# Attention means of two heads taken together, and adaLN column sums taken two by two with their steps dealt out again

## The chip, the cores and the metric

One core of a Trainium2 chip runs the whole program in one launch. The metric is device time in microseconds (us). The core has TensorE (PE in the profile, with PEld for its weight loads), VectorE (DVE), ScalarE (ACT), GpSimd (POOL), SyncE (SP, which here only issues DMAs), and 16 DMA engines.

## The reference, cut to what matters

Two layers over 512 latent tokens and 256 context tokens, 1024 features, 16 heads of 64, float32. Layer 0 mixes tokens by a short gated convolution, layer 1 by neighbourhood attention; each is followed by a SwiGLU of hidden width 2816. Context tokens are carried through layer 0 only.

```
mod   = silu(c)     @ w_ada[i] + b_ada[i]      # 6 vectors of 1024: sh1 sc1 g1 sh2 sc2 g2
mod_c = silu(c_ctx) @ w_ada[i] + b_ada[i]      # the same for context tokens
h = rms_norm(x, norm_mix[i]) * (1 + sc1) + sh1
x = x + g1 * mixer(h)                          # layer 0: conv, layer 1: attention
x = x + g2 * swiglu(rms_norm(x, norm_ffn[i]) * (1 + sc2) + sh2)
# attention, for each head: latent queries on their window and on all context keys
p = softmax(concat(s_win + bias, s_ctx));  o = p_win @ v_win + p_ctx @ v_ctx
```

## The kernel before, in words

Features lie on the 128 partitions (8 tiles), tokens along the free dimension: X is the latent group (512 columns), C the context group (256). A float32 weight tile is split into two float32r parts (`split`: `wh` on ACT at L139, `wl` on DVE at L140), and so is every operand; a product is three matmuls (`mm3`, L193). `Stream` loads weight blocks of 1 MB through SP into a ring of three `raw` buffers and splits one tile ahead.

**Order.** The program is traced once; a planner then simulates it and puts each engine's instructions in an order, in which what was traced earlier goes first when it is ready in the simulation. `in_order` pins an instruction behind everything that was traced before it on its engine. An instruction that is not pinned may be put ahead of one that waits, but once the order is made an engine follows it.

**adaLN (`Ada`).** The product of silu(c) and silu(c_ctx) with w_ada is not done by large matmuls. One step loads 512 rows by 512 columns of w_ada (1 MB, into the same `raw` ring); DVE multiplies by the conditioning column and accumulates into `aa0` (L287, L289), and where context needs it too ACT multiplies (L292, L295) and POOL accumulates into `aa1` (L296). Two steps (halves of the rows) make one piece of 512 columns: half a vector. `flush` sums the piece over the partitions by matmuls against `ones2` (128 rows, 32 columns, one per condition) into 32 partitions of the bank `ada_ps` (L311). After four pieces, two vectors, `finish` copies the bank to `row` on DVE (L318), transposes it (L321), adds the bias, and makes the gains of a norm (1 + scale) * norm weight. The first two vectors of layer 0 are done apart (L241). There are 16 steps for layer 0 and 24 for layer 1 (the last 16 of these without context). In the convolution loop (f = 2 to 7) two steps follow each feature tile, four follow f = 5, and `flush` stands after the first of the three products of the next tile; all 16 are done before the `residual` of the mixer. In the SwiGLU of layer 0 one step follows each hidden tile, two in the first chunk.

**Attention.** Heads go in 8 pairs. For a query tile `b` of 128 queries (4 per pair) and a head `a` of the pair, `scores` makes one bank (L865, L866), its minimum, the bias and mask (L869, L870), the exponential `pt` (L874) and the division (L876, L877); `pt` has two buffers. `mean` transposes four 128-column pieces of `pt` (L893), copies them to `tps` on ACT (L895 to L898), and adds four matmuls of `vv` (128 keys by the 64 columns of this head) with `tps` into the 64 partitions of this head in the bank `op` (L900). At `b` 0 and 3 one of the four has 64 keys only (64 rows). A float32 matmul that isn't a transpose shows as two matmul instructions in the trace, so a head of a query tile has eight at L900. `run` takes (pair, b, a) units in turn: the scores of a unit, then the mean of the unit before, then some steps of `side`, which hold the preparation of the next pair (`operands`) and the projection of the one after (`project`), or in the last two pairs the output projection.

Of the kernel before, what the change touches and what calls it, by code (L numbers as in the profile page):

```python
# [15 lines left out]
P = 128  # L16
# [15 lines left out]
C_ID, C_IND, C_SEL, C_MASK = 0, 128, 160, 288  # L32
MASK_AT = {0: (0, 192), 1: (192, 256), 2: (192, 256), 3: (448, 192)}
C_N = C_MASK + 640
# [3 lines left out]
def dit_kernel(  # L38
# [39 lines left out]
    ct = const.tile([P, C_N], F32, name="ct")  # L78
# [4 lines left out]
    nc.vector.tensor_copy(out=sel, in_=ct[:, C_SEL:C_SEL + P])  # L83
# [12 lines left out]
    cs = const.tile([P, KT, 32], F32, name="cs")  # L96
    nc.vector.memset(cs, 0.0)
    nc.scalar.activation(out=cs[:, :, 0], in_=vt[:, V_C:V_C + KT], func=AF.Silu)
    nc.scalar.activation(out=cs[:, :, 1], in_=vt[:, V_CC:V_CC + KT], func=AF.Silu)
# [114 lines left out]
    class Ada:  # L214


        def __init__(self, pool):
            self.pool = pool
            self.steps = [(i, q, half) for i in range(2) for q in range(4 if i == 0 else 0, 12) for half in range(2)]
            self.pos, self.todo = 0, None  # L220
# [13 lines left out]
        def first_sum(self, n, part, raw):  # L234
# [3 lines left out]
            for j in range(4):  # L238
                for k in range(part * nk, part * nk + nk):
                    kk = k - part * nk  # L240
                    in_order(nc.tensor.matmul(  # L241
                        self.ps[32 * j:32 * j + 32, :wd], cs[:, k, :], raw[:, kk, j // 2, j % 2 * wd:(j % 2 + 1) * wd],
                        start=(k == 0), stop=(k == KT - 1)))
# [20 lines left out]

        def step(self, n=1):
# [5 lines left out]
        def _step(self, i, q, half):  # L271
# [5 lines left out]
            if half == 0:  # L277
                self.flush()
                self.acc = [self.pool.tile([P, 512], F32, name=f"aa{c}", tag=f"aa{c}", bufs=1) for c in range(1 + both)]
            for kk in range(4):  # L280
                k = half * 4 + kk
                for c in range(1 + both):
                    w = cs[:, k, c:c + 1]
# [15 lines left out]
            self.todo = (i, q, both, self.acc)  # L299

        def flush(self):

            if self.todo is None:
                return
            i, q, both, accs = self.todo
            self.todo = None
            j = q % 4
            if j == 0:
                self.ps = bank("ada", "ada_ps")
            for c in range(1 + both):  # L310
                nc.tensor.matmul(self.ps[32 * j:32 * j + 32, :], ones2[:, c, :], accs[c],  # L311
                                 start=(c == 0), stop=(c == both))
            if j == 3:
                self.finish(i, q // 4)

        def finish(self, i, g):
            row = nrm.tile([P, 512], F32, name="row", tag="row", bufs=1)
            nc.vector.tensor_copy(out=row, in_=self.ps)  # L318
            tp = bank("ada", "ada_tp")
            for s in range(4):  # L320
                nc.tensor.transpose(out=tp[:, s * P:(s + 1) * P], in_=row[:, s * P:(s + 1) * P], identity=ident)  # L321
            tv = tp.rearrange("p (s j m) -> p j s m", s=4, j=4)
            ba = vt[:, V_BADA + i * 48 + g * 16:V_BADA + i * 48 + g * 16 + 16].rearrange("p (j s) -> p j s", j=4)
            for cond in range(2 if i == 0 or g == 0 else 1):
                nc.vector.tensor_tensor(
                    out=mod[i][:, cond, g * 16:g * 16 + 16].rearrange("p (j s) -> p j s", j=4),
                    in0=tv[:, :, :, cond], in1=ba, op=ALU.add)
            if g == 1:
                return
            which = 0 if g == 0 else 1  # L330
            base = V_NMIX if which == 0 else V_NFFN
            at = 8 if which == 0 else 32
            gt = const.tile([P, 2, KT], F32, name=f"gain{i}{which}")
            for cond in range(2 if i == 0 or g == 0 else 1):
                nc.vector.scalar_tensor_tensor(
                    out=gt[:, cond, :], in0=mod[i][:, cond, at:at + KT], scalar=1.0,
# [110 lines left out]
    def residual(stream, i, gate, groups, srcs, norms=None, out=None, use="ada"):  # L447
# [18 lines left out]
    def swiglu(tmp, ap_, i, groups, hs, chunks, ada=None, begin=None, norms=None, out=None, end=None, begin_norm=None):  # L466
# [25 lines left out]
        for ci, n_t in enumerate(chunks):  # L492
# [43 lines left out]
            while tt < n_t:  # L536
# [9 lines left out]
                if ada is not None:  # L546
                    ada.step(1 + (ci == 0))
# [4 lines left out]
            residual(st, i, 5, groups, srcs, norms if last else None, out)  # L552
# [3 lines left out]
    with ExitStack() as l0:  # L556
        tmp = l0.enter_context(tc.tile_pool(name="tmp0", bufs=2))
        ap0 = l0.enter_context(tc.tile_pool(name="ap0", bufs=8))
        ada = Ada(tmp)
# [40 lines left out]
        def first_weights(q, j):  # L600
# [3 lines left out]
            elif j == 2:  # L604
                raw = tmp.tile([P, 512], F32, name="fraw", tag=f"aa{q - 2}", bufs=1)
# [467 lines left out]
```

## Time and profile before

| | |
|---|---|
| time, median of 3 runs | 1699.52 us (1699.45 to 1699.55) |
| profiled execution, its own time | 1700.69 us |
| its span, first to last instruction | 1698.6 us |
| PE busy | 1656.7 us (98%) |
| PEld busy | 1366.1 us (80%) |
| DVE busy | 862.5 us (51%) |
| ACT busy | 578.7 us (34%) |
| POOL busy | 245.0 us (14%) |
| mean granted TensorE clock | 0.991 |
| DMA | 162.41 MB, mean 96 GB/s |

Busy is the time in which an engine has at least one instruction under way; for PE that says little about how fast it goes, since matmuls overlap and their ends are modelled. How far apart they start says more.

### The profile page before, as it was taken

Reading aid. Unit: us, or ns where it says so; the run is one execution under the profiler, and the core shown is the slowest. Engines: PE = TensorE matmul, PEld = TensorE weight load, DVE = VectorE, ACT = ScalarE, POOL = GpSimd, SP = SyncE. Lnnn points to the kernel's source line nnn. Section 1 sums busy time; section 2 is a strip of 40 time slices with the busy share of each in tenths; the row PEclk is TensorE's granted clock in tenths of the full one; section 3 lists DMA queues with packets and bytes.
Section 4 is the critical chain, followed back from the end, with each engine's and each line's share of the span. In section 5 each row is a group of like instructions: output and inputs, shape, how many; then the busy total and the mean of one; then the engine's idle time right before and its main releaser. Section 6 shows DMA issues by size and latency. Waiting matters only on the chain.

```text
span 1698.6 us, 22136 instructions
## 1 busy us (share of the span) xinstructions
PE 1656.7 (98%) x9128; PEld 1366.1 (80%) x9128; DVE 862.5 (51%) x1390; ACT 578.7 (34%) x973; POOL 245.0 (14%) x282
## 2 busy tenths in 40 slices
PE   6999989999999999999999999999999999999999
PEld 5887767888788888888888777777778888888887
DVE  5656777267844443234332756555667633333333
ACT  4343333244411211112222555555545522222221
POOL 0134444214500000000003201111120100000000
PEclk9999999999999999999999999999999999999999
DMA  9433434204533333123321211110112023233321
GB/s 303 132 104 122 147 124 149 75 25 150 169 112 101 114 124 124 50 100 124 100 75 50 66 47 57 32 57 26 50 62 82 26 99 111 88 100 99 100 81 68
DMA packets 137076, 162.41 MB, mean 96 GB/s; under 512 B 3216, under 2 KB 114064, under 8 KB 136976
## 3 DMA queue, kind: packets, MB, share of 16 engines
q1 hardware_dynamic: 133504, 156.66, 28.4%
q10 hardware_dynamic: 3472, 4.34, 0.8%
q8 instruction: 71, 1.16, 0.3%
q14 instruction: 29, 0.24, 0.0%
HBM read 158.90 MB, written 2.10 MB: 95 GB/s over the span
## 4 chain that ended last, share of the span: by engine, by line
PE 89%; DVE 7%; DMA 1%; issue 1%; ACT 1%; POOL 0%; SPq 0%; POOLq 0%; DVEq 0%; ACTq 0%
PE ps L193 76%; PE op L900 4%; DVE aa L289 3%; PE tp L893 2%; PE ada_ps L311 2%; DVE wl L140 1%; DMA raw<-in_w_ada_dram 1%; PE s L865 1%; PE ada_ps L241 1%; PE s L866 1%; PE stt L787 1%; DVE al L140 0%; DVE t L426 0%; PE bc L410 0%; DVE hxl L429 0%
## 5 line engine op out<-in xcount | busy, mean ns | idle before, releaser
L193 PE MATMUL ps<-hxh,wh 128*128 128x512 f32 (+1 forms) x1128 | 440.2, 396 | 3.2 <-ACT hxh L428 1.7
L193 PE MATMUL ps<-hxl,wh 128*128 128x512 f32 (+1 forms) x1128 | 434.7, 391 | 1.4 <-DVE hxl L429 1.3
L193 PE MATMUL ps<-hxh,wl 128*128 128x512 f32 (+1 forms) x1128 | 433.6, 390 | 2.4 <-DVE wl L140 2.4
L139 ACT CAST wh<-raw 128x1024 fp32r<-128x1024 f32 (+1 forms) x194 | 198.1, 1023 | 480.4 <-PE ps L193 424.8
L140 DVE TENSOR_TENSOR wl<-raw,wh 128x1024 fp32r<-128x1024 f32 (+1 forms) x194 | 241.0, 1244 | 157.7 <-ACT wh L139 148.0
L193 PEld LDWEIGHTS ps<-hxh,wh 128*128 128x128 f32 x1128 | 212.1, 189 | 66.3 <-issue 10.2
L193 PEld LDWEIGHTS ps<-hxh,wl 128*128 128x128 f32 x1128 | 212.9, 189 | 48.9 <-DVE wl L140 3.5
L193 PEld LDWEIGHTS ps<-hxl,wh 128*128 128x128 f32 x1128 | 212.7, 189 | 46.6 <-DVE hxl L429 3.6
L193 PE MATMUL ps<-ah,wh 128*128 128x512 f32 (+1 forms) x656 | 231.4, 353 | 0.0
L193 PE MATMUL ps<-al,wh 128*128 128x512 f32 (+1 forms) x656 | 230.7, 352 | 0.0
L193 PE MATMUL ps<-ah,wl 128*128 128x512 f32 (+1 forms) x656 | 230.4, 352 | 0.0
L193 PE MATMUL ps<-hch,wl 128*128 128x256 f32 x648 | 181.3, 284 | 0.0
L193 PE MATMUL ps<-hcl,wh 128*128 128x256 f32 x648 | 181.0, 284 | 0.0
L193 PE MATMUL ps<-hch,wh 128*128 128x256 f32 x648 | 179.7, 284 | 0.0
L296 POOL TENSOR_TENSOR aa<-aa,pr 128x512 f32<-128x512 f32 x84 | 132.1, 1573 | 119.5 <-ACT pr L295 62.7
L442 DVE SCALAR_TENSOR_TENSOR x<-ps,mod,x 128x512 f32<-128x512 f32 (+1 forms) x80 | 55.2, 696 | 178.7 <-PE ps L193 178.7
L289 DVE SCALAR_TENSOR_TENSOR aa<-raw,cs,aa 128x512 f32<-128x512 f32 x140 | 139.1, 994 | 7.8 <-DMA raw<-in_w_ada_dram 5.0
L193 PEld LDWEIGHTS ps<-ah,wh 128*128 128x128 f32 x656 | 123.4, 188 | 18.8 <-ACT ah L139 0.8
L193 PEld LDWEIGHTS ps<-ah,wl 128*128 128x128 f32 x656 | 123.4, 188 | 17.5
L193 PEld LDWEIGHTS ps<-al,wh 128*128 128x128 f32 x656 | 123.4, 188 | 17.5
L383 POOL TENSOR_TENSOR acc<-acc,sq 128x256 f32<-128x256 f32 (+1 forms) x40 | 45.9, 1147 | 587.1 <-ACT sq L381 536.6
L485 DVE TENSOR_TENSOR sg<-ps,sg 128x512 f32<-128x512 f32 x66 | 39.7, 601 | 177.2 <-PE ps L193 175.6
(171 smaller groups left out, 1840.1 us busy)
## 6 DMA issues: line engine op xcount, KB each, us to landing
raw<-in_ffn_w_in_dram SPq DMA_DIRECT2D x44, 1024.0 KB, 5.1
raw<-in_w_ada_dram SPq DMA_DIRECT2D x40, 1024.0 KB, 5.1
raw<-in_ffn_w_out_dram SPq DMA_DIRECT2D x16, 1024.0 KB, 4.9
raw<-in_attn_w_qkv_dram SPq DMA_DIRECT2D x12, 1024.0 KB, 5.2
raw<-in_conv_w_in_dram SPq DMA_DIRECT2D x9, 1024.0 KB, 5.2
raw<-in_w_ada_dram SPq DMA_DIRECT2D x16, 512.0 KB, 8.0
raw<-in_ffn_w_out_dram SPq DMA_DIRECT2D x8, 768.0 KB, 4.4
raw<-in_conv_w_out_dram SPq DMA_DIRECT2D x4, 1024.0 KB, 5.2
```

What stands on the lines that cost most here:

```text
L139: a = pinned(nc.scalar.copy(out=hi, in_=src))
L140: b = pinned(nc.vector.tensor_tensor(out=lo, in0=src, in1=hi.bitcast(F32), op=ALU.subtract))
L193: m = nc.tensor.matmul(ps, w[k][part], src[k], start=(first and k == i == 0), stop=(last and k == nk - 1 and i == 2))
L241: in_order(nc.tensor.matmul(self.ps[32 * j:32 * j + 32, :wd], cs[:, k, :], raw[:, kk, j // 2, j % 2 * wd:(j % 2 + 1) * wd], start=(k == 0) ...
L289: nc.vector.scalar_tensor_tensor(out=acc, in0=raw[:, kk, :], scalar=w, in1=acc, op0=ALU.mult, op1=ALU.add)
L296: nc.gpsimd.tensor_tensor(out=acc, in0=acc, in1=pr, op=ALU.add)
L311: nc.tensor.matmul(self.ps[32 * j:32 * j + 32, :], ones2[:, c, :], accs[c], start=(c == 0), stop=(c == both))
L383: eng.tensor_tensor(out=self.a, in0=self.a, in1=sq, op=ALU.add)
L442: nc.vector.scalar_tensor_tensor(out=grp.tiles[f], in0=ps, scalar=modv(i, grp.cond, gate, f), in1=grp.tiles[f], op0=ALU.mult, op1=ALU.add)
L485: nc.vector.tensor_tensor(out=sg, in0=pu[:, :n], in1=sg, op=ALU.mult)
L893: nc.tensor.transpose(out=tp[0:p1, j * P:(j + 1) * P], in_=pt[:, c0:c0 + p1], identity=ident)
L900: nc.tensor.matmul(op_[own, 0:P], vv[p0:p1, vi, own], tps[p0:p1, j * P:(j + 1) * P], start=(j == 0), stop=(j == 3))
```

## The change

Four edits. (1) In attention a unit is now (pair, b) with both heads: both scores, then both heads' transposes (`turned`), one side step, then 8 matmuls in which the heads alternate, each pinned. The 64-row pieces at b = 0 and 3 become full 128-row ones: a value tile with zeros in its other half is added to `vv` (one more transpose per pair). (2) A `flush` waits for two pieces, and their matmuls alternate between the two 32-partition strips, pinned; one vector is then finished alone (10 finishes instead of 5), its bank copied on ACT (64 partitions), with pinned transposes of 64 columns. The accumulators have two sets. (3) The steps are dealt out again: in the convolution one per tile (two at f = 2), four in the mixer's `residual`, the rest along the SwiGLU of layer 0 and in its residuals. In the convolution the flush stands after the second product. (4) `cs` and the raw form of `sel` move to buffers that are reused later.

```diff
-    def residual(stream, i, gate, groups, srcs, norms=None, out=None, use="ada"):
+    def residual(stream, i, gate, groups, srcs, norms=None, out=None, use="ada", along=None):
...
+            if along and f in along:
+                along[f]()
...
+        def also(self):
+            self.flush()
+            self.step()
...
-                self.acc = [self.pool.tile([P, 512], F32, name=f"aa{c}", tag=f"aa{c}", bufs=1) for c in range(1 + both)]
+                self.acc = [self.pool.tile([P, 512], F32, name=f"aa{c}", tag=f"aa{c}{q % 2}", bufs=1) for c in range(1 + both)]
...
-            self.todo = (i, q, both, self.acc)
+            self.todo.append((i, q, both, self.acc))
...
-            if self.todo is None:
+            if len(self.todo) < 2:
                 return
...
             for c in range(1 + both):
-                nc.tensor.matmul(self.ps[32 * j:32 * j + 32, :], ones2[:, c, :], accs[c],
-                                 start=(c == 0), stop=(c == both))
-            if j == 3:
-                self.finish(i, q // 4)
+                for j, (_, _, _, accs) in enumerate(two):
+                    in_order(nc.tensor.matmul(self.ps[32 * j:32 * j + 32, :], ones2[:, c, :], accs[c],
+                                              start=(c == 0), stop=(c == both)))
+            self.finish(i, q // 2)
...
-            nc.vector.tensor_copy(out=row, in_=self.ps)
+            nc.scalar.copy(out=row[0:64, :], in_=self.ps[0:64, :])
             tp = bank("ada", "ada_tp")
             for s in range(4):
-                nc.tensor.transpose(out=tp[:, s * P:(s + 1) * P], in_=row[:, s * P:(s + 1) * P], identity=ident)
+                in_order(nc.tensor.transpose(out=tp[:, s * 64:(s + 1) * 64], in_=row[0:64, s * P:(s + 1) * P],
+                                             identity=ident[0:64, 0:64]))
...
-                ada.step(1 + (ci == 0))
+                ada.step()
...
+            along = {0: ada.also, 2: ada.also, 4: ada.also, 6: ada.flush} if ada is not None and not last else None
+            residual(st, i, 5, groups, srcs, norms if last else None, out, along=along)
...
-        ada.step(2)
+        ada.step()
...
-                if j == 0:
+                if j == 1:
                     ada.flush()
...
-            ada.step(4 if f == 5 else 2)
-        ada.flush()
+            ada.step(2 if f == 2 else 1)
...
-        residual(st, 0, 2, groups, srcs, norms, hs[0])
+        residual(st, 0, 2, groups, srcs, norms, hs[0], along={0: ada.also, 1: ada.also, 2: ada.also, 3: ada.also, 5: ada.flush})
...
+            nc.gpsimd.memset(edge[:, 64:128], 0.0)
+            nc.gpsimd.tensor_copy(out=edge[:, 128:192], in_=vx[:, NX - 64:NX])
...
+            for s, src in enumerate((edge[:, 64:64 + P], v_sb[:, 0:P], v_sb[:, P:2 * P])):
+                nc.tensor.transpose(out=t2[:, s * P:(s + 1) * P], in_=src, identity=ident)
...
+        def turned(b, pt):
+
+            tp = bank("tp", "tp")
+            tps = pa.tile([P, 512], F32, name="tps", tag="tps")
+            for j, (c0, vi) in enumerate(TILES[b]):
+                nc.tensor.transpose(out=tp[:, j * P:(j + 1) * P], in_=pt[:, c0:c0 + P], identity=ident)
+            nc.scalar.copy(out=tps, in_=tp)
+            return tps
+
+        def mean(r, b, tps, op_):
+
+            vv = r["ops"][3]
+            for j, (c0, vi) in enumerate(TILES[b]):
+                for a in range(2):
+                    own = slice(64 * a, 64 * a + 64)
+                    in_order(nc.tensor.matmul(op_[own, 0:P], vv[:, vi, own], tps[a][:, j * P:(j + 1) * P],
+                                              start=(j == 0), stop=(j == 3)))
...
-                    pts[u] = scores(pairs[units[u][0]], *units[u][1:])
+                    pts[u] = [scores(pairs[units[u][0]], units[u][1], a) for a in range(2)]
                 if u > 0:
...
+                    pr, b = units[u - 1]
+                    tps = [turned(b, pt) for pt in pts.pop(u - 1)]
+                    if pos < len(side):
+                        next(side[pos], None)
+                        pos += 1
+                    op_ = bank("op", "op")
+                    mean(pairs[pr], b, tps, op_)
...
-                while pos < min(pace(u), len(side)):
+                while pos < min(pace(2 * u + 1), len(side)):
```

## Rows read from the trace of the kernel before

**Rows 1.** The chain that ended last: its shares of the span by line.
```profile
by line: PE ps L193 76.1%; PE op L900 3.9%; DVE aa L289 2.7%; PE tp L893 1.8%; PE ada_ps L311 1.7%; issue 1.3%; DVE wl L140 1.2%; DMA raw<-in_w_ada_dram 1.2%; PE s L865 1.2%; PE ada_ps L241 1.2%; PE s L866 0.9%; PE stt L787 0.6%; DVE al L14
```

**Rows 2.** Tiles op, ada_ps: matmuls, count, shortest/median/longest ns, first and last start.
```profile
L900 PE MATMUL op<-tps,vv x512: 269/273/324, 1001.5 to 1323.5; 128*64 128x128 f32 x150, 64*64 64x128 f32 x21
...
L311 PE MATMUL ada_ps<-aa,ones x64: 592/617/1062, 71.7 to 839.5; 128*32 128x512 f32 x64
```

**Rows 3.** Timeline of PE, attention of one pair: start, length (us), what.
```profile
1059.70 1.58 PE L900 MATMUL op<-tps,vv 128*64 128x128 f32 x16
...
1069.97 0.28 PE L193 MATMUL ps<-hch,wh 128*128 128x256 f32 x1
1070.18 1.09 PE L900 MATMUL op<-tps,vv 128*64 128x128 f32 x8
1071.20 0.39 PE L193 MATMUL ps<-hcl,wh 128*128 128x256 f32 x1
1071.42 0.28 PE L193 MATMUL ps<-hch,wl 128*128 128x256 f32 x1
1071.54 0.27 PE L193 MATMUL ps<-hch,wh 128*128 128x256 f32 x1
```

**Rows 4.** The stretch of 16 at 1059.70, L900 alone, by windows: matmuls under way (x).
```profile
1059.69:1060.18 0.49, 0.48 (x4) 0.48 (x5) 1.00 0.00 0
1060.18:1060.62 0.44, 0.44 (x10) 0.44 (x9) 1.00 0.00 0
```

**Rows 5.** Timeline of PE: sums of three 32-column matmuls in three strips.
```profile
1073.77 0.62 PE L787 MATMUL stt<-sq,ct 128*32 128x512 f32 x2
1073.78 0.62 PE L787 MATMUL stt<-sqc,ct 128*32 128x512 f32 x1
...
1074.76 0.50 PE L865 MATMUL s<-ks,qh 128*128 128x512 f32 x1
```

**Rows 6.** Timeline of PE around adaLN sums (L311), at three places.
```profile
135.53 1.91 PE L311 MATMUL ada_ps<-aa,ones 128*32 128x512 f32 x2 [3.29 <-DVE aa L289]
...
138.39 0.63 PE L193 MATMUL ps<-hxh,wl 128*128 128x512 f32 x1
138.82 0.63 PE L193 MATMUL ps<-hxh,wh 128*128 128x512 f32 x1
...
287.08 1.90 PE L311 MATMUL ada_ps<-aa,ones 128*32 128x512 f32 x4
...
540.64 1.04 PE L311 MATMUL ada_ps<-aa,ones 128*32 128x512 f32 x2
```

**Rows 7.** Waits of PE from 60 to 300 us: in total, times, longest.
```profile
PE ada_ps L311 <- DVE aa L289: 14.5, 4, 4.6
```

**Rows 8.** Windows after those waits (first, and sum of four): engines' busy, PEclk.
```profile
134.80:141.60 6.80, 6.07 (x11) 2.52 (x11) 4.69 (x7) 2.27 (x3) 0.00 (x0) 0.50 0.54 184
...
sum 23.90, PE 20.69 PEld 9.46 DVE 12.59 ACT 6.64 POOL 3.31; mean PE 5.17 PEld 2.36 DVE 3.15 ACT 1.66 POOL 0.83
```

**Rows 9.** Groups: DVE from 480 to 850 us, from 180 to 290; POOL.
```profile
L289 DVE SCALAR_TENSOR_TENSOR aa<-raw,cs,aa 128x512 f32<-128x512 f32 x49 | 36.8, 750 | 2.1 <-DMA raw<-in_w_ada_dram 0.8
...
L289 DVE SCALAR_TENSOR_TENSOR aa<-raw,cs,aa 128x512 f32<-128x512 f32 x33 | 42.4, 1285 | 2.0 <-DMA raw<-in_w_ada_dram 1.4
...
L296 POOL TENSOR_TENSOR aa<-aa,pr 128x512 f32<-128x512 f32 x84 | 132.1, 1573 | 119.5 <-ACT pr L295 62.7 <-ACT aa L292 52.6
```

**Rows 10.** Windows: the mixer's residual, the first SwiGLU chunk with its steps, and attention.
```profile
295.00:353.00 58.00, 58.00 (x329) 50.57 (x328) 16.44 (x24) 13.26 (x20) 15.03 (x11) 1.00 0.17 55
...
375.00:470.00 95.00, 93.50 (x510) 75.62 (x510) 75.61 (x84) 46.12 (x72) 44.91 (x28) 1.00 0.46 150
...
958.00:1326.00 368.00, 366.79 (x2176) 287.03 (x2175) 223.32 (x537) 192.16 (x398) 53.79 (x93) 1.00 0.17 53
```

**Rows 11.** Groups of ACT and DVE in attention, 1050 to 1215 us.
```profile
L874 ACT ACTIVATE pt<-s,mn 128x512 f32<-128x512 f32 (+1 forms) x32 | 21.4, 670 | 9.5 <-DVE mn L870 9.4
...
L877 DVE TENSOR_SCALAR pt<-pt,mn 128x448 f32<-128x448 f32 (+1 forms) x31 | 14.4, 465 | 1.0
```

More of the change, by code (lines that the diff above doesn't have):

```diff
@@ L77, in dit_kernel @@
     nc.sync.dma_start(out=vt, in_=vec)
-    ct = const.tile([P, C_N], F32, name="ct")
+    ct = const.tile([P, C_SEL], F32, name="ct")
     nc.scalar.dma_start(out=ct[:, :C_MASK], in_=cst[:, :C_MASK])
@@ L82, in dit_kernel @@
     sel = const.tile([P, P], F32R, name="sel")
-    nc.vector.tensor_copy(out=sel, in_=ct[:, C_SEL:C_SEL + P])
+    sel_raw = nrm.tile([P, P], F32, name="sel_raw", tag="y", bufs=1)
+    nc.scalar.dma_start(out=sel_raw, in_=cst[:, C_SEL:])
+    nc.vector.tensor_copy(out=sel, in_=sel_raw)
     ones = const.tile([P, 32], F32, name="ones")
@@ L325, in finish @@
+            conds = range(2 if i == 0 or g < 2 else 1)
+            for cond in conds:
                 nc.vector.tensor_tensor(
-                    out=mod[i][:, cond, g * 16:g * 16 + 16].rearrange("p (j s) -> p j s", j=4),
+                    out=mod[i][:, cond, g * 8:g * 8 + 8].rearrange("p (j s) -> p j s", j=2),
                     in0=tv[:, :, :, cond], in1=ba, op=ALU.add)
-            if g == 1:
+            if g not in (1, 4):
                 return
-            which = 0 if g == 0 else 1
+            which = 0 if g == 1 else 1
@@ L331, in finish @@
             base = V_NMIX if which == 0 else V_NFFN
-            at = 8 if which == 0 else 32
             gt = const.tile([P, 2, KT], F32, name=f"gain{i}{which}")
-            for cond in range(2 if i == 0 or g == 0 else 1):
+            for cond in conds:
                 nc.vector.scalar_tensor_tensor(
-                    out=gt[:, cond, :], in0=mod[i][:, cond, at:at + KT], scalar=1.0,
+                    out=gt[:, cond, :], in0=mod[i][:, cond, g * 8:g * 8 + 8], scalar=1.0,
                     in1=vt[:, base + i * KT:base + (i + 1) * KT], op0=ALU.add, op1=ALU.mult)
@@ L558, in dit_kernel @@
         ap0 = l0.enter_context(tc.tile_pool(name="ap0", bufs=8))
-        ada = Ada(tmp)
+        cs = tmp.tile([P, KT, 32], F32, name="cs", bufs=1)
+        nc.vector.memset(cs, 0.0)
+        nc.scalar.activation(out=cs[:, :, 0], in_=vt[:, V_C:V_C + KT], func=AF.Silu)
+        nc.scalar.activation(out=cs[:, :, 1], in_=vt[:, V_CC:V_CC + KT], func=AF.Silu)
+        ada = Ada(tmp, cs)
         load_set()
@@ L980, in dit_kernel @@
             ops, prj = operands(pairs[pr + 1]), project(pr + 2, pairs[pr + 2])
-            run([(pr, b, a) for b in range(4) for a in range(2)], [ops, prj, ops, prj, prj, ops] + [prj] * 17,
+            run([(pr, b) for b in range(4)], [ops, prj, ops, prj, prj, ops] + [prj] * 17,
                 lambda u: 2 * (u + 1) + u // 2)
@@ L1002, in dit_kernel @@
         ops, outs, ld, nxt = operands(pairs[KT - 1]), out_first(), load_last(), after_a()
-        run([(pr, 2 * h + b, a) for h in range(2) for pr in (KT - 2, KT - 1) for b in range(2) for a in range(2)],
+        run([(pr, 2 * h + b) for h in range(2) for pr in (KT - 2, KT - 1) for b in range(2)],
             [ops, outs, ops, outs, outs, ops] + [outs] * 5 + [ld, outs, outs] * 8 + [nxt] * 19, lambda u: 5 * (u + 1) // 2 + u // 2)
```

82 lines of the change are left out of this document (25 added, 57 removed).

## The prediction

> **What bounds the kernel now.** I read the page's busy table first, then the chain of waits, then the timeline of PE where the change works. The busy table puts PE at 98%, and the chain agrees: three quarters of the span are the products at L193, and what the change touches on PE is small beside them, L900 with 3.9% and L311 with 1.7% [rows 1]. The reader is to see that no other engine holds the end as a whole, so that a microsecond of PE saved is one saved, wherever PE does not stand. Where it stands the waits tell: from 60 to 300 us PE waits 14.5 us in four places for the adaLN accumulation, up to 4.6 us at a time [rows 7], and behind each of these waits the granted clock is 0.50, which is 1.2 GHz of 2.4, for 23.9 us together [rows 8]. In attention PE is busy 366.8 of 368 us, DVE 223 and ACT 192 [rows 10]: it is bound by PE alone.
>
> **Means by turns.** 512 instructions at L900 [rows 2] are 64 groups of eight, one for each head of a query tile. On the chain they take 3.9% of 1698.6 us, 66.2 us [rows 1]. That leaves out what a group costs its neighbours. From 1069.97 to 1071.42 there are a 256-column product, a lone group and one more product: 1.45 us, less twice the 0.12 by which such products follow each other (1071.42 to 1071.54), is 1.21, of which 1.02 (1070.18 to 1071.20) is the group and 0.19 its entry and exit [rows 3]. The groups lie in 53 stretches in the timeline (the first at 1001.5, the last at 1322.5), so before they cost 66.2 + 53 x 0.19 = 76.3 us. After there are 32 stretches of 16. Do two heads run beside each other? At 1059.70 two groups stood together: 16 instructions in 1.58 us where a lone eight takes 1.09 [rows 3], and inside it, once the second head's operand had come, 10 were under way in 0.44 us where in the 0.49 before only 4 were [rows 4]. Three 32-column sums in three strips tell the same: 0.99 us for all three [rows 5], while one alone takes 1.04 [rows 6]. So I take 1.21 for a stretch of 16: 32 x 1.21 = 38.7, a gain of 37.6 us. The other end is no overlap: 32 x (16 x 0.1275 + 0.19) = 71.4, a gain of 5. The 64-row pieces become full ones, which costs no columns. Eight more transposes, at no more than the 0.12 of a 256-column product, add 1.
>
> **The unit of two heads.** Two scores are made before the two means of the unit before, but `pt` still has two buffers, so the exponential of a unit now waits for the transposes of the unit before. Queued behind it on ACT are the weight casts and projection copies. From transposes to the next transposes there lie at least an exponential of 0.67 and a division of 0.47 for each head [rows 11], some 2.3 us for two. A unit has about (368 - 37) / 32 = 10.3 us of PE work [rows 10], most of it projection that nothing here holds up, and the planner may put it ahead. So I hold it hidden; unhidden it costs 32 x 2.3 = 74. I add 2 for the last units, where less work lies beside them (0 to 5).
>
> **Sums by turns.** 64 instructions at L311 [rows 2] are 32 matmuls. They lie in 27 stretches (first 71.7, last 839.0): 22 with one matmul, 1.04 each, and 5 with two, 1.90 [rows 6]. With the 0.19 of entry and exit from above, less 0.07 that the length overlaps what follows (1.09 against 1.02), a stretch is 1.16 or 2.02: 35.6 us. After, six flushes have four matmuls in two strips, two deep, so 2.02, and four have two in two strips, 1.16: 16.8. Gain 18.8; without overlap only the 17 fewer stretches are saved, 17 x 0.12 = 2. Ten finishes take the place of five: no row has a 64-by-64 transpose, so I bound five more finishes by nothing and by five of 4 x 0.13 + 0.19 with as much again for a change of shape, 7; I take 3.5, the middle, since no nearer row decides. The copy of the bank goes from DVE to ACT, off the path.
>
> **Steps spread.** In the convolution two steps a tile become one, and the flush comes one product later: 24 x (0.23 + 0.12) = 8.4 us more lead for work cut by half, so the four waits go: 14.5 [rows 7]. With them goes the lower clock. PE worked 20.7 of the 23.9 us [rows 8]; a 512-column product took 0.43 there (138.39 to 138.82 [rows 6]) against some 0.23 at 2.4 GHz, so 20.7 x (1 - 0.23/0.43) = 9.6 us come back (0 to 12). Next late is the `residual` of the mixer: four steps, one per tile of 8.4 us. It has 58 us with DVE at 16.4 and POOL at 15.0 over eight tiles [rows 10], that is 2.1 and 1.9 a tile. A step adds four accumulations, 0.75 each alone and 1.29 when POOL works beside them, and on POOL four of 1.57 [rows 9]: DVE 5.1 to 7.2, POOL 8.2. It just fits. The first SwiGLU chunk had the same rate before, and PE stood 1.5 us in 95 [rows 10]. Behind a slow step stand on ACT and DVE the splits of the next weights, which are one tile ahead. The bounds are 0 and 8 (POOL's 8.2 of one tile laid open once); I take 4.
> The Trainium skill, "SBUF — State Buffer", section "SBUF: two separate sides", speaks against this edit: DVE reading two SBUF operands and POOL reading SBUF exclude each other for a whole instruction. By it 5.1 and 8.2 would add up to 13.3 a tile, 4.9 too much, some 20 us over four tiles. The trace agrees that the accumulation slows beside POOL (0.75 to 1.29), not that such a rate holds PE up: the chunk had it, with 75.6 + 44.9 us of DVE and POOL in 95, at 1.5 us of PE [rows 9, 10].
> The rest of the steps have 16.8 us each in the SwiGLU. The last one, though, now follows the last hidden tile, with the flush right behind it and no product between. PE then either takes the residual's products first or waits as in rows 7, 3.6 on average, plus the lower clock: 0 to 7, I take 3. Raw `sel` is a second DMA behind which DVE's first copy waits at the start: -0.5 to 1.5, I take 0.5.
>
> **Sum.** -37.6 + 1 + 2 - 18.8 + 3.5 - 14.5 - 9.6 + 4 + 3 + 0.5 = -66.5 us. The profiled execution took 1700.7 us, of which the span is 1698.6; the median of the runs is 1.2 us lower, 1699.5, and from that I subtract: 1633.
>
> **Rivals.** First, the waits move instead of going: the residual, or the late flush, holds PE as the convolution did, and with it the clock falls. Against it stands the chunk of rows 10; for it, that POOL fits with nothing left. It gives back 14.5 + 9.6: 1657. Second, the halves don't run beside each other when they alternate: the gains of 37.6 and 18.8 shrink to 5 and 2, 1682. Rows 4 and 5 are against it. A rule of the Trainium skill would bring it about: "TensorE: Matmul & The Clock Gate", Part 3, says weight loads overlap running matmuls only where the row group differs, and both heads use all 128 rows; the trace disagrees, with 10 in 0.44 us. Third, slower than before: the wait for `pt`. If the planner leaves PE standing between a unit's scores and its transposes, each unit pays; from 66.5 / 32 = 2.1 us a unit the change loses, and with the unhidden 2.3 it ends at 1633 + 74 = 1707, later still if the clock falls in the gaps. For it is the ring of two; against it are products that wait for nothing in each unit.
>
> **How the numbers follow.** Forecast 0.77, first rival 0.13, second 0.04, third 0.04, and 0.02 for a mixture that ends where it began. The forecast's own range is 1616 (residual, late flush, finishes, last units and the start at their lower ends, the clock at 12) to 1650 (the same at their upper ends). The range of 1616 to 1660 takes in the first rival. A measurement of this kernel can tell 0.2%, 3.4 us: faster 0.94, within 0.02, slower 0.04.
>
> **What would show it.** L900 in 32 stretches of 16, each near 1.1 us; L311 in ten stretches, of 2 and 1.1 us; no wait of PE for `aa` before 300 us and the clock at 1.0 from 110 us on; attention some 35 us shorter. Wrong would be: stretches of 16 that take 2.2 us, a PE idle behind `pt`, or a clock under 1.0 in the residual or at the end of layer 0's SwiGLU.

## The result, and the profile after

The changed kernel takes 1640.1 us, median of four runs (1639.0 to 1641.3), against 1699.5 us before (1699.45 to 1700.1, four runs beside it): a ratio of 0.965, 95% interval 0.9633 to 0.9667. The forecast was 1633 with a range of 1616 to 1660, its own range 1616 to 1650. The gain is 59.4 us where 66.5 were forecast. The profiled execution has a span of 1637.2 us, 61.4 below that of before; the account of the terms below is made against these 61.4.

The page of the kernel after: busy time of each engine, and further down the chain of waits by line, which answers to [rows 1]. L900 is now L908, L311 is L313, L289 is L292.
```profile
PE 1607.5 (98%) x9156; PEld 1344.5 (82%) x9156; DVE 859.5 (52%) x1393; ACT 578.3 (35%) x967; POOL 242.9 (15%) x290
...
PE ps L192 83%; PE op L908 2%; PE tp L898 2%; PE ada_ps L240 1%; PE s L878 1%; DMA raw<-in_w_ada_dram 1%; PE ada_ps L313 1%; PE s L879 1%; PE stt L795 1%; DVE wl L139 1%; DVE t L428 0%; DVE aa L292 0%; PE bc L412 0%; DVE hxl L431 0%; DMA x<-in_xT_dram 0%
```
PE still holds nearly all of the chain. The large products went from 76% of it to 83%, the means (L908) from 3.9% to 2%, the column sums (L313) from 1.7% to 1%, and DVE's `aa` from 2.7% to under 1%: what left the chain are the three things that the forecast named.

**The means.** Timeline of PE in the kernel after, one unit of two heads (start, length in us, what), and the same kernel 24 us later.
```profile
1073.65 1.09 PE L908 MATMUL op<-tps,vv 128*64 128x128 f32 x16
1074.67 0.50 PE L192 MATMUL ps<-hxh,wh 128*128 128x512 f32 x1
...
1097.26 0.43 PE L908 MATMUL op<-tps,vv 128*64 128x128 f32 x2
1097.62 0.50 PE L878 MATMUL s<-ks,qh 128*128 128x512 f32 x1
...
1098.75 1.09 PE L908 MATMUL op<-tps,vv 128*64 128x128 f32 x14
1099.77 0.77 PE L898 MATMUL tp<-ct,pt 128*128 128x128 f32 x5
```
The first unit is what was forecast: 16 instructions from 1073.65 to 1074.67, in the 1.02 us that eight of full rows took before [rows 3]. The second is not: two instructions stand alone, then four score products, then the other 14. The 14 still take 1.02 us, because eight of them belong to the second head and set the length; the two that stand apart are pure loss. They take 0.36 us (1097.26 to 1097.62) and add an entry and an exit of 0.19. Of the 32 units 20 are parted in this way, which makes 20 x 0.55 = 11 us.

**The 64-row pieces.** What a head took before hung on its rows. Four pieces of the chain of the kernel before: start, us, what.
```profile
1001.61 2.32 PE op L900 x16
1008.11 1.51 PE op L900 x16
1070.25 1.02 PE op L900 x8
1076.16 1.16 PE op L900 x8
```
A lone head took 1.02 us when all its pieces had 128 rows (18 heads) and 1.16 us when one had 64 (25 heads). Two heads next to each other took 1.51 us with full rows (seven times); with a 64-row piece in each they took 2.32 us (three times), twice 1.16, so that they did not overlap at all. The zero rows of edit 1 are therefore more than a convenience: by these numbers they alone save 25 x 0.14 + 3 x 0.81 = 5.9 us of what the means gained. The forecast says only that they cost no columns; its 66.2 us for the means of before hold the 5.9. No run has the turns without the full rows, so how much the units at b = 0 and 3 would overlap without them is not shown.

The two tiles of [rows 2] in the kernel after: matmuls, count, shortest/median/longest ns, first and last start.
```profile
L908 PE MATMUL op<-tps,vv x512: 272/273/324, 961.8 to 1262.0; 128*64 128x128 f32 x171
...
L313 PE MATMUL ada_ps<-aa,ones x64: 592/592/617, 159.2 to 827.3; 128*32 128x512 f32 x64
```
The count of instructions is the same at both lines, and the length of one is the same at L908 and nearly so at L313. What was gained lies in how many are under way together, which neither count nor mean length shows. The timeline shows it, and so does the time in which at least one is under way: 69.8 us at L900, 43.5 at L908; 37.3 at L311, 15.7 at L313. From first to last the means take 300 us where they took 322.

**The sums.** Timeline of PE in the kernel after: a flush of two pieces, and the transposes of its finish.
```profile
159.25 1.91 PE L313 MATMUL ada_ps<-aa,ones 128*32 128x512 f32 x8
161.09 0.50 PE L192 MATMUL ps<-hxh,wh 128*128 128x512 f32 x1
...
166.66 0.28 PE L192 MATMUL ps<-hch,wh 128*128 128x256 f32 x1
166.87 0.46 PE L322 MATMUL ada_tp<-ct,row 64*128 64x64 f32 x4
167.25 0.39 PE L192 MATMUL ps<-hcl,wh 128*128 128x256 f32 x1
167.47 0.28 PE L192 MATMUL ps<-hch,wl 128*128 128x256 f32 x1
```
Eight instructions take 1.91 us by their length, where four took 1.90 [rows 6]; start to start they take 1.84. The finish is 0.38 us of transposes (0.39 in most of the ten). The product before it is followed after 0.21 us instead of 0.12, and the one behind it after 0.22: 0.09 of entry and 0.10 of exit. The five finishes of before were transposes of the full 128 by 128; they took 0.35 us, with no entry and 0.08 of exit. So most of the exit is not the price of a smaller tile, and the entry is.

**The waits.** PE's waits from 60 to 300 us, first the kernel before (the one above 1 us beside the row of `aa` in [rows 7]), then the kernel after: engine, line, what it waited for, us in total, times, longest.
```profile
PE ps L193 <- DVE wl L140: 1.9, 1, 1.9
```
```profile
PE ps L192 <- ACT hxh L430: 0.5, 1, 0.5
```
Windows of the kernel before and of the kernel after, from 63 to 300 us: length, busy of PE, PEld, DVE, ACT and POOL with counts, granted clock, DMA share, GB/s.
```profile
63.00:300.00 237.00, 220.09 (x1174) 176.62 (x1172) 170.86 (x214) 85.89 (x131) 95.00 (x100) 0.94 0.36 119
```
```profile
63.00:300.00 237.00, 236.55 (x1397) 205.44 (x1395) 161.60 (x211) 86.19 (x132) 85.73 (x96) 1.00 0.35 115
```
In the same 237 us PE now starts 1397 matmuls instead of 1174, at a granted clock of 1.00 instead of 0.94. The four waits and the 1.2 GHz that followed them [rows 7, 8] are gone. A fifth wait went with them, 1.9 us for a weight part on DVE, which the forecast had not counted.

**One new wait.** PE's waits over the whole span of the kernel after, three of its rows.
```profile
PE ps L192 <- ACT ah L138: 2.7, 1, 2.7
PE s L878 <- ACT pt L887: 1.8, 5, 1.0
...
PE ps L192 <- DVE al L139: 0.3, 1, 0.3
```
The first and the third are one event, at 432 us, in the last hidden tile of the first SwiGLU chunk. Timelines of PE, ACT, DVE and POOL in the kernel after; in brackets the idle time before, and what ended it.
```profile
432.31 0.28 PE L192 MATMUL ps<-ah,wl 128*128 128x256 f32 x1
435.29 0.42 PE L192 MATMUL ps<-ah,wh 128*128 128x256 f32 x1 [2.70 <-ACT ah L138]
436.06 0.58 PE L192 MATMUL ps<-al,wh 128*128 128x256 f32 x1 [0.34 <-DVE al L139]
...
436.65 0.63 PE L192 MATMUL ps<-ah,wh 128*128 128x512 f32 x1
```
```profile
434.83 0.41 ACT L138 CAST ah<-sg 128x256 fp32r<-128x256 f32 x1 [3.06 <-DVE sg L489]
```
```profile
427.35 3.49 DVE L292 SCALAR_TENSOR_TENSOR aa<-raw,cs,aa 128x512 f32<-128x512 f32 x2
430.76 2.04 DVE L139 TENSOR_TENSOR wl<-raw,wh 128x768 fp32r<-128x768 f32 x1
432.72 1.75 DVE L292 SCALAR_TENSOR_TENSOR aa<-raw,cs,aa 128x512 f32<-128x512 f32 x1
434.39 0.41 DVE L489 TENSOR_TENSOR sg<-ps,sg 128x256 f32<-128x256 f32 x1
434.73 0.94 DVE L139 TENSOR_TENSOR wl<-raw,wh 128x768 fp32r<-128x768 f32 x1
```
```profile
426.93 6.99 POOL L299 TENSOR_TENSOR aa<-aa,pr 128x512 f32<-128x512 f32 x4 [3.70 <-ACT pr L298]
```
Read backwards: PE waits for `ah`, ACT's cast of `ah` waits for `sg` on DVE, and `sg` stands in DVE's queue behind accumulations of an adaLN step that take 1.75 us each, and a weight split between them that takes 2.04. POOL accumulates beside them until 433.9 us, 1.75 us each as well. Without POOL the same split takes 0.94 (434.73), and of the 140 accumulations of this kernel the 81 that have no POOL instruction beside them take 0.74 to 0.76. Behind the wait the granted clock is 0.51, the lower of its two levels, from 435.4 to 438.9 us; a 512-column product then takes 0.63 us by its length, 0.43 start to start (436.65 to 437.08). The wait costs 2.9 us (432.31 to 435.29, less the 0.12 of the product), the clock some 1.7, half of 3.4: 4.6 us.

### The profile page after: what moved, and what is told of

Read it like the earlier page. It is cut to its first block, busy times and chain, and to the rows that moved or that the text cites. A ratio compares the mean times of both kernels' runs of the same rounds, so it can differ in the third digit from the quotient of the medians.

```text
span 1637.2 us, 22217 instructions
## 1 busy us (share of the span) xinstructions
PE 1607.5 (98%) x9156; PEld 1344.5 (82%) x9156; DVE 859.5 (52%) x1393; ACT 578.3 (35%) x967; POOL 242.9 (15%) x290
## 4 chain that ended last, share of the span: by engine, by line
PE 93%; DVE 3%; ACT 1%; DMA 1%; issue 1%; POOL 0%; SPq 0%; POOLq 0%; DVEq 0%; ACTq 0%
PE ps L192 83%; PE op L908 2%; PE tp L898 2%; PE ada_ps L240 1%; PE s L878 1%; DMA raw<-in_w_ada_dram 1%; PE ada_ps L313 1%; PE s L879 1%; PE stt L795 1%; DVE wl L139 1%; DVE t L428 0%; DVE aa L292 0%; PE bc L412 0%; DVE hxl L431 0%; DMA x<-in_xT_dram 0%
## 5 line engine op out<-in xcount | busy, mean ns | idle before, releaser
L192 PE MATMUL ps<-hxh,wh 128*128 128x512 f32 (+1 forms) x1128 | 435.4, 392 | 3.5 <-ACT hxh L430 1.7
L192 PEld LDWEIGHTS ps<-hxl,wh 128*128 128x128 f32 x1128 | 211.2, 188 | 43.5 <-DVE hxl L431 3.2
L292 DVE SCALAR_TENSOR_TENSOR aa<-raw,cs,aa 128x512 f32<-128x512 f32 x140 | 144.5, 1033 | 40.9 <-DMA raw<-in_w_ada_dram 37.8
L192 PEld LDWEIGHTS ps<-hch,wh 128*128 128x128 f32 x648 | 122.1, 191 | 4.4 <-issue 1.9
L192 PEld LDWEIGHTS ps<-hcl,wh 128*128 128x128 f32 x648 | 122.8, 191 | 1.9
```

Of the source, the lines that this page charges most:

```text
L192: m = nc.tensor.matmul(ps, w[k][part], src[k], start=(first and k == i == 0), stop=(last and k == nk - 1 and i == 2))
L292: nc.vector.scalar_tensor_tensor(out=acc, in0=raw[:, kk, :], scalar=w, in1=acc, op0=ALU.mult, op1=ALU.add)
```

## The experiments

The theory: the time is the sum of a part in attention, where alternation of the heads halves the means but not quite a third of that is lost where units are parted, and a part in adaLN, where halving the steps per tile takes the waits away. The rivals stand with each experiment. Behind each time stand its ratio to the kernel before, run beside it, and the 95% interval of that ratio.

**The attention edit alone, and the adaLN edits alone.** The first is the kernel before with edit 1, that is with `TILES`, `turned`, `mean`, `run` and `vv` of the kernel after, and with the moved buffers of edit 4 that make room for it:

> The kernel before with the attention edit alone (units of two heads, means by turns, the full-row edge tiles, and the buffers moved to make room); adaLN as before. Theory, from the trace after: in 20 of the 32 units the first matmul pair of the means stands apart from the other 14 instructions, so the means hold PE 32 x 1.21 + 20 x 0.55 = 49.9 us instead of 76.3; less 1 for the transposes and some 4 for new short waits in attention the gain is 21: 1678 us. Rival: the splits come from how the adaLN edit shifts the planner's order, and alone the attention edit gives what was forecast, 37.6 - 1 - 2: 1665 us.

The second is the kernel after with `mean`, `run` and `vv` of the kernel before:

> The changed kernel with the attention of before: adaLN edits alone. Theory, the two parts add up: the attention edit alone gave 20 of the 59 us, so this gives 39: 1660 us. Rival: the parts share gains (the planner's order, the clock), and this is 5 us or more off that: under 1655 or over 1665.

The first took 1680.1 us (0.988, 0.9869 to 0.9898), the second 1661.4 (0.979, 0.9763 to 0.9817). Their gains are 20 and 37 us and add up to 57 of the 59 of both: within the noise of the runs the parts do not touch each other. With the attention edit alone, too, 20 of the 32 units are parted, so the parting does not come from the adaLN edits. Attention was worth 20 us and not the 35 that the forecast had for it (-37.6 + 1 + 2); adaLN was worth 37 where its other terms make 32.

**The second head first.** The head whose transposed operand comes last begins the pinned chain, so that nothing of a unit can start before all of it can:
```diff
             for j, (c0, vi) in enumerate(TILES[b]):
-                for a in range(2):
+                for a in (1, 0):
```


> The changed kernel with the heads of the means in the order second, first. The pinned chain then begins with the head whose operand is copied last, so nothing can be put between its first matmul and the rest. Theory: 32 stretches of 16 instructions, 20 x (0.36 + 0.19) = 11 us less, 1629 us. Rival: the first pair was issued early only because the other operand was late, so PE now waits for that copy in each unit, and the time stays at 1640 us.


It took 1631.9 us (0.960, 0.9588 to 0.9617). All 32 units have their 16 together; timeline of PE in this kernel:
```profile
1086.58 1.09 PE L908 MATMUL op<-tps,vv 128*64 128x128 f32 x16
1087.61 0.65 PE L898 MATMUL tp<-ct,pt 128*128 128x128 f32 x4
```
8 us of the 11 came back. PE's waits in attention, 955 to 1270 us, of this kernel tell of the rest:
```profile
PE s L878 <- ACT pt L887: 3.5, 6, 1.0
PE ps L192 <- DVE q_sb L846: 1.1, 1, 1.1
```
The waits for `pt` grew from 1.8 to 3.5 us and that for `q_sb` in attention from 0.3 to 1.1: PE, done sooner with the means, stands for the next operands. In the profiled execution the clock takes a part as well: it is at 0.50 for 3.4 us from 1195.5 us on, behind the wait for `q_sb`, and for 6.8 us instead of 3.4 behind the wait at 434 us, which this kernel still has. So the parted units come from the order that the planner chose, given a chain whose first link needed one head alone: cause shown, and three quarters of its cost.

**Head by head.** Both operands are awaited as before, but the second head's four matmuls stand together, then the first head's (against the kernel of the experiment before):
```diff
-            for j, (c0, vi) in enumerate(TILES[b]):
-                for a in (1, 0):
+            for a in (1, 0):
+                for j, (c0, vi) in enumerate(TILES[b]):
```


> As the run with the second head first, but without turns: the four matmuls of the second head, then the four of the first, pinned and next to each other. Theory one: PE runs matmuls of the two 64-column halves beside each other whenever they stand next to each other in its queue, whatever their order (before, at 1059.7 us, the second head's joined the first's though they were queued behind all of them): same as that run, 1629 us. Theory two: the alternation is what makes them overlap: 32 x (16 x 0.1275 + 0.19 - 1.21) = 33 us more, 1662 us.


It took 1647.7 us (0.970, 0.9681 to 0.971), which neither side expected. Timeline of a unit, start and length:
```profile
1091.89 1.58 PE L908 MATMUL op<-tps,vv 128*64 128x128 f32 x16
1093.40 0.77 PE L898 MATMUL tp<-ct,pt 128*128 128x128 f32 x5
```
Windows of L908 alone, busy of PE and PEld with the matmuls under way (x), here:
```profile
1091.89:1092.37 0.48, 0.48 (x4) 0.48 (x5) 1.00 0.00 0
1092.37:1092.86 0.49, 0.49 (x10) 0.49 (x9) 1.00 0.00 0
```
and in the kernel with the second head first:
```profile
1086.58:1087.06 0.48, 0.48 (x8) 0.48 (x10) 1.00 0.00 0
```
With the heads in blocks a unit takes 1.51 us (1091.89 to 1093.40). Four of the first block's eight instructions run alone, and the other head's first starts with the fifth; by turns the heads run together from the start, 8 in the first 0.48 us. 32 x (1.51 - 1.02) = 15.7 us, and the two kernels differ by 15.7. This is also the picture of [rows 4]: 4 in 0.49 us, then 10 in 0.44, and all seven pairs of full-row heads that stood together there took 1.51 us. So in the kernel before, too, the second head did not start late for want of its operand, as the forecast read it, but because it stood eight instructions back.

**Two and two.** If PE reaches four instructions ahead, blocks of two matmuls (four instructions) of each head should lose almost nothing (against the kernel after):
```diff
-            for j, (c0, vi) in enumerate(TILES[b]):
-                for a in range(2):
+            for j2, a, j1 in [(j2, a, j1) for j2 in range(2) for a in (1, 0) for j1 in range(2)]:
+                for j, (c0, vi) in [(2 * j2 + j1, TILES[b][2 * j2 + j1])]:
```


> As the run with the second head first, but the heads alternate after two matmuls each (four instructions in the trace). In the head-by-head run the other head's first instruction started with the fifth of eight, at a cost of 0.49 us a unit. Theory: PE begins a matmul on the other half only when at most four instructions are queued ahead of it; then blocks of four overlap as fully as single turns: stretches of 1.02 us, 1632 us. Rival: the head start is half of any block, whatever its length: two instructions lost twice a unit, some 0.2 to 0.4 us x 32, 1639 to 1645 us.


It took 1632.0 us (0.962, 0.9594 to 0.9638), the same as turns of one. Timeline of a unit:
```profile
1087.59 1.15 PE L908 MATMUL op<-tps,vv 128*64 128x128 f32 x16
1088.66 0.77 PE L898 MATMUL tp<-ct,pt 128*128 128x128 f32 x5
```
1.07 us start to start against 1.02 by turns and 1.51 in blocks of eight. That agrees with a reach of four instructions, counted from the one that starts; blocks of six were not tried.

**The sums strip by strip.** The same question for the flush, where a strip has two matmuls, four instructions:
```diff
-            for c in range(1 + both):
-                for j, (_, _, _, accs) in enumerate(two):
+            for j, (_, _, _, accs) in enumerate(two):
+                for c in range(1 + both):
```


> The changed kernel with the adaLN sums strip by strip instead of by turns, all else as changed: at most four instructions for a strip stand ahead of the other strip's. Theory, a look-ahead of four instructions: the strips overlap as before the edit, flushes of 1.84 and 0.98 us, 1640 us. Rival, the alternation is needed: six flushes of 3.4 and four of 1.9, 13 us more, 1653 us.


1639.8 us (0.966, 0.9639 to 0.9684), as the kernel after. A flush takes 1.84 us from 158.67 on, as by turns:
```profile
158.67 1.92 PE L313 MATMUL ada_ps<-aa,ones 128*32 128x512 f32 x8
160.51 0.50 PE L192 MATMUL ps<-hxh,wh 128*128 128x512 f32 x1
```
Here the gain came from two pieces in one flush, not from the turns.

**The steps where they were.** The kernel after with the steps and flushes at the places of before (two steps a tile in the convolution, four at f = 5, two a tile in the first chunk, the flush after the first product, nothing in the residuals; a flush still takes two pieces):
```diff
-                if j == 1:
+                if j == 0:
                     ada.flush()
...
-            ada.step(2 if f == 2 else 1)
+            ada.step(4 if f == 5 else 2)
...
-                    ada.step()
+                    ada.step(1 + (ci == 0))
...
-            along = {0: ada.also, 2: ada.also, 4: ada.also, 6: ada.flush} if ada is not None and not last else None
+            along = None
...
```


> The changed kernel with the adaLN steps and the flush where they were before (two steps per tile in the convolution, four at the sixth, the flush after the first product, none in the residuals). Theory: the waits of 14.5 us and the lower clock's 9.6 come back, and the 4.6 us of the new wait at 432 us go: 1660 us. Rival: the second set of accumulators, the sums by turns and ACT's copy take most of the waits away by themselves: 1640 to 1645 us.


1665.9 us (0.981, 0.9791 to 0.9824): 26 us of the gain lie in where the steps stand. PE's waits from 60 to 300 us in this kernel:
```profile
PE ada_ps L313 <- DVE aa L292: 7.3, 3, 3.3
PE ps L192 <- DVE a L601: 3.3, 1, 3.3
PE ps L192 <- DVE wl L139: 3.1, 1, 3.1
PE ada_ps L313 <- POOL aa L299: 2.0, 2, 1.3
...
```
15.7 us of waits are back, 9.3 of them at the flush and 6.4 for other work of DVE that is queued behind the accumulations. With them the clock is at 0.50 again, in five stretches of 20.5 us together, in which PE works 18.6; as in the forecast that costs some 8.6 us. The loss is 6 us above the theory's: it had left out a wait as the one at 97 us of the kernel before, which is here 3.1 us (the third row), with 6.8 us of the lower clock behind it. The rival holds in part: at the flush 9.3 us are left of 14.5, but the sum of the waits is nearly that of before (14.5 + 1.9).

**The flush after the first product again.** Of the two things that changed at once in the convolution, steps halved and flush later, the second alone undone:
```diff
-                if j == 1:
+                if j == 0:
                     ada.flush()
```


> The changed kernel with the convolution's flush back after the first product of a tile; the steps stay spread. It tells which half of the edit took the four waits away. Theory, the number of steps: with one step a tile the sums are ready within one product, 1640 us and no wait at L313. Rival, the later flush: PE waits again for aa at the one flush that lies in the convolution, 3 to 5 us with the lower clock, 1644 us.


1641.4 us (1638.9 to 1642.5; 0.965, 0.9641 to 0.9668): no difference. PE's waits from 60 to 300 us are one row, 0.5 us for `hxh`, the same as in the kernel after. So halving the steps took the four waits away; the later flush was not needed.

**Both faults mended.** The second head first, and the first chunk's last step moved: none after its last hidden tile, where the wait of 432 us arose, and the steps that follow at f = 1, 3, 5, 7 of the chunk's residual instead of 0, 2, 4:
```diff
-                for a in range(2):
+                for a in (1, 0):
...
-                if ada is not None:
+                if ada is not None and not (ci == 0 and tt == n_t - 1):
                     ada.step()
...
-            along = {0: ada.also, 2: ada.also, 4: ada.also, 6: ada.flush} if ada is not None and not last else None
+            along = dict({1: ada.also, 3: ada.also, 5: ada.also, 7: ada.also} if ci == 0 else {0: ada.also, 2: ada.also, 4: ada.also, 6: ada.flush}) if ada is not None and not last else None
```


> The second head first, and the steps of the first SwiGLU chunk moved: none after its last hidden tile, four in its residual after the tiles 1, 3, 5 and 7. Theory: PE's wait of 2.9 us at 432 us for the last tile's operand came from that step's accumulations on DVE, which POOL slows, ahead of the tile's own gate; without it the wait and its slow clock go, 6 us in the run with the second head first: 1626 us. Rival: the crowding only moves into the residual, 1632 us.


1626.3 us (1624.5 to 1627.2; 0.958, 0.9557 to 0.9603), 73 us below the kernel before and 14 below the kernel after: the best version of this study. Windows from 420 to 445 us, first in the kernel after, then in this one:
```profile
420.00:445.00 25.00, 21.96 (x129) 19.33 (x128) 14.66 (x17) 9.27 (x14) 9.83 (x7) 0.93 0.45 147
```
```profile
420.00:445.00 25.00, 25.00 (x159) 22.57 (x158) 13.45 (x17) 7.53 (x12) 5.84 (x4) 1.00 0.46 147
```
PE is idle for 3.0 of the 25 us in the one and never in the other, which starts 30 more matmuls. Against the kernel with the second head first alone (1631.9) the moved steps are worth 5.6 us, where 4.6 were read for the wait and its clock in the kernel after. In the profiled execution of this version the clock does not fall at all between 25 us and the end of the span.

**Three banks for scores.** What holds PE in attention now are the waits for `pt`. If they came from too few score banks, a third one, taken from the transposes, would help:
```diff
-    deal(mm=[0, 1, 2], s=[3, 4], tp=[5, 6], op=[7])
+    deal(mm=[0, 1, 2], s=[3, 4, 5], tp=[6], op=[7])
```


> The run with both repairs (second head first, steps moved), with three PSUM banks for scores and one for the transposes instead of two and two. In attention PE now waits for ACT's exponential before a score matmul, 3.5 us in six places, because the two score banks hold the unit before. Theory one, the banks are the limit: those waits go, 1623 us. Theory two, the limit is the exponential itself, which waits for a buffer of pt until the transposes of the unit before have run: another bank frees nothing, and the single transpose bank makes the second head's transposes wait for the first's copy, covered by products: 1626 to 1632 us.


1635.2 us (0.962, 0.9608 to 0.9634), 9 slower than the version it started from; the first theory expected a gain, the second a loss of 6 at most. PE's waits over the whole span:
```profile
PE op L908 <- ACT tps L899: 5.2, 5, 1.2
...
PE tp L898 <- ACT tps L899: 2.3, 5, 0.7
PE s L878 <- ACT pt L887: 1.8, 3, 0.8
```
The waits for `pt` did fall, from 3.5 to 1.8. But with one bank for transposes the second head's transposes wait for ACT to copy the first head's out (2.3), and the means for the second copy (5.2). These two waits are over four times the 1.7 us that were gained. Besides, 4 of the 32 units are parted again, at some 2 us.

## Why the prediction was right, and where its terms were off

The mechanism held, the time lay in the range, and none of the three rivals came true at its price. By its own steps, with what the trace of after shows against each term:

| term | forecast, us | shown, us |
|---|---|---|
| means by turns | -37.6 | -37.6 + 11 |
| transposes | +1 | +1 |
| last units and new waits in attention | +2 | +4 |
| sums by turns | -18.8 | -18.8 |
| five more finishes | +3.5 | +3.6 |
| four waits for `aa` | -14.5 | -14.5 |
| lower clock behind them | -9.6 | -9.6 |
| two waits not counted, 97 and 426 us, and the clock behind the first | 0 | -4.4 |
| residual | +4 | 0 |
| late last flush | +3 | 0 |
| wait at 432 us and its clock | 0 | +4.6 |
| start | +0.5 | 0 |
| sum | -66.5 | -60.7 |

The two profiled executions differ by 61.4, so 0.7 us stay open. The rows on the clock are worked out and not measured apart: 20.7 us of work at 0.50 as in the forecast, and 3.4 us of work at 0.50 from 100.7 to 104.1 us beside waits of 1.9 and 0.9. That the forecast missed by only 7 us of 66 is in part luck. The parted units, the other losses in attention and the wait at 432 us cost 17.6 us more than it had; the waits it had not counted, and a residual, a late flush and a start that cost nothing, gave 11.9 back. The ends of its own range do not come out of its bounds exactly either: they add up to 1617 and, with the clock's term left as it is, to 1648.5.

**The step that was mis-sized is "after there are 32 stretches of 16".** The price of a stretch was right to the hundredth, 1.02 us and 0.19. The count was not: 20 units fell into two stretches, which makes 52. (The 53 stretches of before are 55 in the timeline, since one head was parted there too; that is 0.4 us.) The forecast treated the pinned matmuls as one block. A pin gives an order and no more: each matmul starts when its own operand is there, and the first needed one head's transposes alone. The planner put it ahead and filled the gap to the second with other products. That the first matmul depends on less than the others could be read in `mean` before the run; the kernel with the second head first shows that this was the cause.

**"Once the second head's operand had come"** was a wrong reading of [rows 4] that did no harm to the sum. In the head-by-head kernel the first head's operand is there when the second head's block starts, and the block behind still joins with the fifth instruction, at the same 0.49 us. So the place in the queue was the cause. It matters because by the forecast's reading the order within a unit would be free: it is worth 16 us.

**The wait for `pt`** is 1.8 us in five places of the kernel after, not 2.3 in each of 32 units: the planner hid it, as the forecast held. The other 2 us of that row I read from the starts of PE's instructions around the `bc` products (L844, L845), whose two halves the transposes now often part, each with an entry and an exit of its own; no experiment isolates them.

**The residual and the late flush** cost nothing, and neither does the flush anywhere: L313 waits in no place of the kernel after. The first rival, that waits move instead of going, came true once and small, in a place that the forecast did not name: not the flush and not the residual, but `sg` in DVE's queue behind an adaLN step. For the residual the forecast named the weight splits that stand behind a step; for the SwiGLU it asked only whether the accumulations end in time for the flush, and not who stands behind them on DVE. In the kernel with the old steps, too, 6.4 of the 15.7 us of waits are of that kind.

**The weight loads.** The second rival is settled: 16 instructions of two heads take the 1.02 us of eight. The Trainium skill, "TensorE: Matmul & The Clock Gate", Part 3, says that weight loads overlap running matmuls only where the row group differs. Both heads use all 128 rows, and PEld is busy in all of the 0.48 us in which eight of their matmuls start, so the measurement decides against the rule here. What the trace adds is that the order decides how much overlaps: 1.02, 1.07 and 1.51 us for turns of one, of two and of four matmuls.

**DVE beside POOL.** The 1.29 us that the forecast took for an accumulation beside POOL is a mean of two kinds [rows 9]: of those 33, 14 take 0.74 to 0.75 us and 19 take 1.44 to 1.79. At 432 us both engines' accumulations take 1.75 us each while they run side by side. The Trainium skill, "SBUF — State Buffer", section "SBUF: two separate sides", calls the pair of ports that the two engines share an exclusive lock. The trace is nearer to that than the forecast allowed: the two engines fall into one step, though a shorter one than the 2.04 us that 0.75 and POOL's shortest accumulation, 1.29, make end to end. In one place it held PE up for 3 us. Over the mixer's residual, where by that rule 20 us were at stake, PE is not held: no wait of PE lies between 255 and 320 us, and the clock is at 1.00.

**Left open.** What is left on PE in attention of the best version are 3.5 us of waits for `pt` and 1.1 for `q_sb`. Whether the first come from the ring of two or from ACT's queue is not settled. A third buffer for `pt` was not tried.

## What to carry to other kernels

When two column halves of PE are to run together, alternate them matmul by matmul (or in blocks of at most two float32 matmuls), let all their pieces have the same rows, and begin with the one whose operand comes last: a pinned chain is parted where its first link is ready early, and the parts cost more than their share. Spread background work so that what is issued at once is short against the lead of whoever is queued behind it on the same engine; here halving what was issued at once took away every wait for it in the convolution, and moving its due date did nothing. Read such a gain from the timeline: count and mean length of the means, and PE's busy share of 98%, were the same before and after.

## What the runs showed of the hardware

- Two heads of full rows in the two column halves of PE overlap wholly by turns (16 instructions in 1.02 us), but only from the fifth instruction on when eight of one head stand first (1.51 us); in blocks of four instructions 1.07 us.
- One 64-row piece among 128-row ones lengthens a head from 1.02 to 1.16 us, and two such heads next to each other, 2.32 us, do not overlap.
- A stretch in a smaller tile of PE costs 0.19 us of entry and exit beside its own length: four 64-by-64 transposes of 0.38 us pay it as 16 matmuls of 1.02 do. Four full 128-by-128 transposes pay no entry and 0.08 of exit.
- A wait of 3.0 us at 432 us is followed by a granted clock of 0.51 for 3.5 us, so it costs 4.6. In the kernel with the second head first the clock stays low for 6.8 us there, and a wait of 1.1 us at 1195 us is followed by 3.4 us at 0.50; in the version with both faults mended the same wait, at 1189 us, is not.
- DVE's two-operand accumulation takes 0.74 to 0.76 us alone; side by side with POOL's, both take 1.75 us each. A weight split of DVE takes 2.04 us there instead of 0.94.
